# First weights in halves, later head tables, and a plan that knows where the rounded weights lie

## The chip, the cores and the metric

The kernel runs on one core of one Trainium2 chip. Its time is the device time of one execution in microseconds (us). The core has five engines that run their own instruction streams in order and wait for one another by semaphores: TensorE (PE in the profile; its weight loads are PEld), VectorE (DVE), ScalarE (ACT), GpSimd (POOL) and SyncE (SP), which issues DMAs.

## The reference, cut to what matters

Two layers of a streaming encoder run on 512 prompt rows and 64 sample rows of 1024 features with the same weights. The sample group has 1024 cached keys. In each layer:

```python
h = rms_norm(x, norm_g)
u_p, z_p, q, k, v, qi, ki, wi, z_a, g_p, g_a = split(h @ w_in)
br_pool = (pool_mix(u_p) * silu(z_p)) @ w_pool_out     # means over 2, 4, 8, 16 rows, mixed by groups
q, k, qi, ki = rope(q), rope(k), rope(qi), rope(ki)
score = sum_heads(wi * relu(qi . ki));  sel = top_k(score)      # 128 of the prompt's keys, 256 of the sample's
o = softmax(q . k[sel]) . v[sel]
br_attn = (o * silu(z_a)) @ w_attn_out
x = x + (sigmoid(g_p) * br_pool + sigmoid(g_a) * br_attn) @ w_o
```

After the second layer x is normed once more. The outputs are y, the new k, v and indexer keys, and the last rows of the pooling input.

## The kernel before

**Tiling.** Everything lies transposed: features on the 128 partitions, the 576 rows (T) along the free dimension, in two halves of 288. x is eight blocks of 128 x 576. A weight piece is a tile of 128 x 1024 (512 KB); a layer has 58 of them, and one piece makes one "block" of the product: eight steps k, each with three matmuls for each half of the rows. They make up an f32 product from rounded parts: high weights by high x, high weights by low x, low weights by high x (`step`). High parts are cast by ScalarE; the low part of x is a subtraction on VectorE. The low part of a weight piece is, from the third piece on, made by a DMA that GpSimd issues and that adds the raw tile to the negated high part (`split_to`). The first two pieces are rounded in halves: ScalarE casts 512 columns, then VectorE (first half) or GpSimd (second half) subtracts (`split_first`). Raw tiles (`raw`) and rounded tiles (`whl`) have three places each, so piece i + 2 is rounded into the place of piece i - 1.

**Order.** A Python planner writes the instruction streams out when the program is built. Main work is emitted in the order of `ORDER` (u, z, the gates gp with the pool output po, then k, q, v, then za, ga). Side work (pooling, scores, selection, attention, rounding of what comes next) is written as generators; after each step of a product `plan.pump()` looks which generators may go on. `need(engine, tiles)` says yes if by the plan's clocks the tiles are ready and, where a `room` is given, the engine's backlog is no more than that many microseconds. The plan's clocks are estimates of each engine's free time (`plan.free`), and `plan.wrote` and `plan.last` keep when a tile is written and last used. Tiles taken through `plan.slot` know when their place comes free; the `whl` tiles are not taken so. `plan.finish` pumps until given generators are done.

**Weights.** `weights()` hands out the next piece and loads three ahead. `block()` takes the piece, calls `split_to(i + 3)`, which puts the rounding of piece i + 2 into ScalarE's stream, and then emits the eight steps.

**The start of layer 0.** SP issues gains, the ki weights, x blocks 0 and 1, the whole first weight piece, x blocks 2 to 7. `arrive(k)` (line 1465) calls `first` (line 498): ScalarE scales block k into its high part, VectorE makes the low part; at k = 0 the ki weights are split (`ki_split`); at k = 1 the first weights are rounded; at k = 7 all eight blocks are squared on ScalarE and the squares summed by seven additions on VectorE. The loop of line 580 runs the ki product and the first product side by side; with `LAG` = (1, 2) the high-weight matmuls of step k - 1 and the low-weight matmuls of step k - 2 follow the ki matmuls of block k. Blocks 0 to 2 arrive ahead of the loop, and turn k brings block k + 2. At the end of turn 4 weight piece 1 is rounded (line 599), at the end of turn 6 piece 2. The second product (line 611 on) uses piece 1; after its third step come the norm's ten matmuls (`norm_a`), after its fifth the transposes that spread the result over Rt (`norm_b`). The rotary tables, and all that leaves a product, are multiplied by Rt.

**Head tables.** `head_tables` (line 968) loads the cosine and sine tables of the heads and multiplies them by Rt with two GpSimd instructions into Ct and St. It is started at the first gate block (gp 0, line 1324). k and q use the tables.

Nearly every instruction goes through the helper at line 262, so rows are told apart by tiles.

Of the kernel before, what the change touches and what calls it, by code (L numbers as in the profile page):

```python
# [10 lines left out]
F32 = mybir.dt.float32  # L11
F32R = mybir.dt.float32r
AF = mybir.ActivationFunctionType
OP = mybir.AluOpType

P = 128
# [30 lines left out]
UNITS = 3  # L47
FIRST_H = ()
LAG = (1, 2)
DMA_US = 3.0  # L50
WARM = 11
NORM_A = 0
# [215 lines left out]
def encoder_step(ctx: ExitStack, tc: tile.TileContext, a: dict):  # L268
# [60 lines left out]
    for l in range(DEPTH):  # L329
        pieces += [(l, j) for j in range(a["n_pieces"])]  # L330
    raw_of, split_of = {}, {}
    state = {"load": 0, "split": 0, "next": 0}

    def load_to(n):
        while state["load"] < min(n, len(pieces)):
# [3 lines left out]
            dma.dma_start(raw_of[i], a["w"][l, j])  # L339
            state["load"] += 1  # L340

    def split_to(n):
        while state["split"] < min(n, len(pieces)):
            i = state["split"]
            load_to(i + 1)
            x = raw_of.pop(i)
            w = rot.tile([P, 2, 1024], F32R, name="whl", tag="whl", bufs=3)
            act.copy(w[:, 0], x)

            act.activation(w[:, 1], x, AF.Copy, scale=-1.0)  # L350
            pool.dma_start(w[:, 1].bitcast(F32), x, accum_op=OP.add)
            plan.let(x)
            split_of[i] = w
            state["split"] += 1

    def split_first(i=0):

        load_to(i + 1)
        x = raw_of.pop(i)
        w = rot.tile([P, 2, 1024], F32R, name="whl", tag="whl", bufs=3)  # L360
        for c, eng in ((slice(0, 512), dve), (slice(512, 1024), pool)):
            act.copy(w[:, 0, c], x[:, c])
            eng.tensor_tensor(w[:, 1, c], x[:, c], w[:, 0, c].bitcast(F32), op=OP.subtract)
        plan.let(x)
        split_of[i] = w
        state["split"] = i + 1

    def weights():
        i = state["next"]
# [83 lines left out]
            if True in low:  # L453
                pe.matmul(o, lhsT=wl, rhs=h, start=False, stop=k == nk - 1)

    def product(ps, w, xh, xl, nk, off=0):
        for k in range(nk):
            step(ps, w, xh, xl, k, nk, off)
            plan.pump()

    def block(xh, xl, nk=8):
        w, i = weights()
        split_to(i + 3)
        ps = ps_mm()
        product(ps, w, xh, xl, nk)
        return ps

    class Entry:
# [29 lines left out]
        def first(self, k, x, ki_split):  # L498

            c = slice((k % 2) * T, (k % 2 + 1) * T)  # L500
            g = gains[:, self.l, k:k + 1]
            h = self.h[k // 2][:, c]
            if k in FIRST_H:
                dve.tensor_scalar(h, x, g, None, op0=OP.mult)
            else:
                act.activation(h, x, AF.Copy, scale=g)
            if k == 0:
                ki_split()
            dve.scalar_tensor_tensor(self.lo[k // 2][:, c], x, g, h.bitcast(F32), op0=OP.mult, op1=OP.subtract)
            self.rest.append(x)  # L510
            if k == 7:
                for i, x in enumerate(self.rest):
                    sq = tmp() if i else self.acc
                    act.activation(sq, x, AF.Square)
                    if i:
                        dve.tensor_tensor(self.acc, sq, self.acc, op=OP.add)
# [38 lines left out]
    def layer(l, x, arrive):  # L555
# [6 lines left out]


        if l == 0:
            for k in range(3):
                arrive(k)
        w, n = weights()
        if l:
# [11 lines left out]
        for k in range(8 + lag[1]):  # L580
            if k == 7:
                plan.finish(*x.coming)
            if 3 <= k + 2 < 8:
                arrive(k + 2)
            if k < 8:
                c = (k % 2) * T
                for s in range(2):
                    cols = slice(c + s * HT, c + (s + 1) * HT)
                    pe.matmul(ps_k[s][:, :HT], lhsT=kiw[:, k], rhs=xh[k // 2][:, cols], start=k == 0, stop=False)
                for s in range(2):  # L590
                    cols = slice(c + s * HT, c + (s + 1) * HT)
                    pe.matmul(ps_k[s][:, :HT], lhsT=kiw[:, k], rhs=xl[k // 2][:, cols], start=False, stop=k == 7)
            if lag[0] <= k < 8 + lag[0]:
                step(ps_q0, w, xh, xl, k - lag[0], 8, low=(False,))
            if k >= lag[1]:
                step(ps_q0, w, xh, xl, k - lag[1], 8, low=(True,))
                plan.pump()
            if l == 0 and k == 4:
                split_first(1)
            if l == 0 and k == 6:  # L600
                split_to(3)
# [718 lines left out]
        for name, i in ORDER:  # L1320
            if name == "k" and i == 0:
                att = start(attend(), 3)
            if name == "gp" and i == 0:
                start(head_tables(), 2)
            jobs[name](i)
        plan.finish(sel)
# [131 lines left out]
    for k in range(8):  # L1458
        if k % 2 == 0:
            xt.append(quart())  # L1460
        dma.dma_start(xt[-1][:, (k % 2) * T:(k % 2 + 1) * T], a["x"][k])
        if k == 1:
            load_to(1)

    def arrive(k):
        x.first(k, xt[k // 2][:, (k % 2) * T:(k % 2 + 1) * T], ki_split)
        if k == 7:
            plan.let(*xt)
        if k == 1:
            split_first()  # L1470

    x = layer(0, x, arrive)
    for l in range(1, DEPTH):
# [107 lines left out]
```

## Time and profile before

| what | us |
|---|---|
| median of 3 runs | 920.47 (920.26 to 920.74) |
| the profiled execution | 921.1 |
| its span, first to last instruction | 919.3 |
| TensorE busy | 894.8 |
| VectorE busy | 668.3 |
| ScalarE busy | 593.2 |
| GpSimd busy | 202.1 |

Engines work side by side, so busy times don't add up. A row of a timeline gives the start, how long the instruction (or the run of like instructions, x their number) took, the engine, the operation with what it writes and reads, and in brackets how long the engine had been idle before and what ended that. The granted clock of TensorE was 0.995 of full speed on average.

### The profile page before, as it was taken

Reading aid. Unit: us, or ns where it says so; the run is one execution under the profiler, and the core shown is the slowest. Engines: PE = TensorE matmul, PEld = TensorE weight load, DVE = VectorE, ACT = ScalarE, POOL = GpSimd, SP = SyncE. Lnnn points to the kernel's source line nnn. Section 1 sums busy time; section 2 is a strip of 40 time slices with the busy share of each in tenths; the row PEclk is TensorE's granted clock in tenths of the full one; section 3 lists DMA queues with packets and bytes.
Section 4 is the critical chain, followed back from the end, with each engine's and each line's share of the span. In section 5 each row is a group of like instructions: output and inputs, shape, how many; then the busy total and the mean of one; then the engine's idle time right before and its main releaser. Section 6 shows DMA issues by size and latency. Waiting matters only on the chain.

```text
span 919.3 us, 17403 instructions
## 1 busy us (share of the span) xinstructions
PE 894.8 (97%) x6613; PEld 881.4 (96%) x6613; DVE 668.3 (73%) x1554; ACT 593.2 (65%) x1056; POOL 202.1 (22%) x217
## 2 busy tenths in 40 slices
PE   8999999999999999999999999999999999999996
PEld 7999999999999999999999999999999999999995
DVE  6996899799896677362359779988989875755314
ACT  7556534588898975564537564446889988556642
POOL 3111211134432300112211121113443222011121
PEclk9999999999999999999999999999999999999998
DMA  7756587766555675779976667786655548648862
GB/s 266 187 140 164 134 214 189 173 161 160 125 145 147 179 199 150 186 202 240 263 191 175 154 151 163 191 203 180 165 139 133 157 124 221 189 135 222 236 146 104
DMA packets 54500, 160.97 MB, mean 175 GB/s; under 512 B 6736, under 2 KB 9040, under 8 KB 54416
## 3 DMA queue, kind: packets, MB, share of 16 engines
q0 software_dynamic: 16416, 59.78, 34.8%
q1 hardware_dynamic: 38000, 100.08, 32.2%
q8 instruction: 52, 0.85, 0.4%
q14 instruction: 32, 0.26, 0.1%
HBM read 85.37 MB, written 14.69 MB: 109 GB/s over the span
## 4 chain that ended last, share of the span: by engine, by line
PE 68%; DVE 14%; ACT 13%; issue 3%; DMA 1%; POOL 1%; SPq 0%; DVEq 0%; ACTq 0%; POOLq 0%
PE mm L262 57%; PE sm L262 11%; DVE tmp L262 6%; DVE quart L262 6%; ACT prob L262 4%; ACT whl L262 3%; ACT quart L262 2%; ACT qz L262 1%; ACT L262 1%; DVE big L262 1%; ACT tmp L262 1%; POOL tmp L262 1%; DMA raw<-in_w_dram 1%; DMA prob<-in_c_v_dram 1%; DVE prob L262 0%
## 5 line engine op out<-in xcount | busy, mean ns | idle before, releaser
L262 PE MATMUL mm<-quart,whl 128*128 128x288 f32 (+1 forms) x5568 | 780.4, 296 | 1.6 <-ACT quart L262 1.2
L262 PEld LDWEIGHTS mm<-quart,whl 128*128 128x128 f32 x5568 | 754.2, 188 | 4.3 <-ACT quart L262 2.0
L262 POOL DMA_DIRECT2D whl<-raw x114 | 99.3, 871 | 648.9 <-ACT whl L262 433.1
L262 ACT CAST whl<-raw 128x1024 fp32r<-128x1024 f32 (+1 forms) x118 | 121.8, 1034 | 133.2 <-PE mm L262 88.7
L262 ACT ACTIVATE whl<-raw 128x1024 fp32r<-128x1024 f32 x114 | 120.4, 1056 | 0.0
L262 ACT ACTIVATE prob<-prob,stat 128x128 f32<-128x128 f32 (+3 forms) x128 | 67.5, 554 | 6.8 <-DVE stat L262 6.4
L262 DVE SCALAR_TENSOR_TENSOR quart<-prob,wcol,quart 128x256 f32<-128x256 f32 (+4 forms) x60 | 42.1, 704 | 26.4 <-ACT prob L262 25.1
L262 ACT ACTIVATE prob<-sm 128x256 f32<-128x256 f32 (+4 forms) x72 | 33.5, 481 | 38.4 <-PE sm L262 38.4
L262 DVE MATCH_REPLACE8 quart<-stat,quart 128x256 f32<-128x256 f32 (+2 forms) x96 | 51.1, 539 | 0.0
L262 DVE MAX8 stat<-quart 128x8 f32<-128x256 f32 (+2 forms) x96 | 47.3, 541 | 0.0
L262 DVE MAX8 quart<-quart 128x8 f32<-128x544 f32 x64 | 46.3, 723 | 1.2
L262 DVE MATCH_REPLACE8 quart<-quart 128x544 f32<-128x544 f32 x64 | 45.4, 709 | 0.0
L262 DVE TENSOR_TENSOR tmp<-tmp 128x576 f32<-128x576 f32 (+7 forms) x62 | 44.3, 720 | 1.3
L262 DVE TENSOR_TENSOR quart<-quart 128x576 fp32r<-128x576 f32 (+6 forms) x30 | 26.4, 881 | 21.5 <-ACT quart L262 21.0
L262 DVE TENSOR_TENSOR big<-sm,big 128x512 fp32r<-128x512 f32 (+1 forms) x64 | 28.9, 483 | 16.3 <-ACT big L262 16.1
L262 ACT CAST quart<-tmp 64x512 fp32r<-64x512 f32 (+4 forms) x44 | 24.1, 566 | 22.0 <-POOL tmp L262 11.7
L262 ACT COPY prob<-sm 64x512 f32<-64x512 f32 (+1 forms) x24 | 12.3, 514 | 39.0 <-PE sm L262 38.6
L262 PE MATMUL sm<-quart,big 128*128 128x128 f32 (+3 forms) x176 | 32.2, 291 | 1.4 <-DVE tmp L262 1.4
L262 ACT CAST big<-sm 128x512 fp32r<-128x512 f32 (+2 forms) x72 | 28.0, 434 | 8.4 <-PE sm L262 8.0
L262 DVE SCALAR_TENSOR_TENSOR quart<-tmp,gains,quart 128x576 fp32r<-128x576 f32 x8 | 6.5, 818 | 31.6 <-ACT quart L262 31.6
L262 DVE CUSTOM_DVE_ANT_0 prob<-sm,quart 128x512 f32<-128x512 f32 (+2 forms) x48 | 25.8, 550 | 4.8 <-PE sm L262 4.8
L262 DVE TENSOR_TENSOR quart<-mm,tmp 128x576 f32<-128x576 f32 (+2 forms) x10 | 6.4, 638 | 29.3 <-PE mm L262 29.3
(157 smaller groups left out, 1025.5 us busy)
## 6 DMA issues: line engine op xcount, KB each, us to landing
raw<-in_w_dram SPq DMA_DIRECT2D x116, 512.0 KB, 4.9
whl<-raw POOLq DMA_DIRECT2D x114, 512.0 KB, 4.8
mp<-tmp SPq DMA_DIRECT2D x16, 288.0 KB, 3.3
tmp<-mp SPq DMA_DIRECT2D x16, 288.0 KB, 4.7
prob<-in_c_k_dram SPq DMA_DIRECT2D x16, 256.0 KB, 4.8
prob<-in_c_v_dram SPq DMA_DIRECT2D x16, 256.0 KB, 3.8
out_o_v_dram<-quart SPq DMA_DIRECT2D x8, 320.0 KB, 4.6
quart<-in_x_dram SPq DMA_DIRECT2D x8, 288.0 KB, 6.3
```

Source lines behind the costliest of these rows:

```text
L262: return f(*args, **kw)
```

## The change

It has four parts.

1. The first weight piece is fetched as two halves, one behind x block 1 and one behind x block 3, and each half is rounded when block 1 or block 3 has been scaled (`load_half`, `split_half`). Four blocks instead of three arrive ahead of the loop, and turn k brings block k + 3 instead of k + 2. The ki weights are split ahead of block 0's scaling.
2. The head tables are started at gate block `TABLES_AT` = 6 instead of 0.
3. `whls` makes the rounded tiles and tells the plan that a tile's place is free when the tile three before has been used for the last time.
4. In `block()`, the rounding of piece i + 2 is emitted after step `SPLIT_AT` = 0 and the pump behind it, instead of ahead of the eight steps.

```diff
 UNITS = 3
 FIRST_H = ()
 LAG = (1, 2)
+TABLES_AT = 6
+SPLIT_AT = 0
 DMA_US = 3.0
 WARM = 11
 NORM_A = 0
@@ -329,6 +331,7 @@
     for l in range(DEPTH):
         pieces += [(l, j) for j in range(a["n_pieces"])]
     raw_of, split_of = {}, {}
+    whl_names = []
     state = {"load": 0, "split": 0, "next": 0}
 
     def load_to(n):
@@ -339,12 +342,20 @@
             dma.dma_start(raw_of[i], a["w"][l, j])
             state["load"] += 1
 
+    def whls(i):
+
+        w = rot.tile([P, 2, 1024], F32R, name="whl", tag="whl", bufs=3)
+        whl_names.append(w.tensor.name)
+        if i > 2:
+            plan.wrote(w, plan.last[whl_names[i - 3]])
+        return w
+
     def split_to(n):
         while state["split"] < min(n, len(pieces)):
             i = state["split"]
             load_to(i + 1)
             x = raw_of.pop(i)
-            w = rot.tile([P, 2, 1024], F32R, name="whl", tag="whl", bufs=3)
+            w = whls(i)
             act.copy(w[:, 0], x)
 
             act.activation(w[:, 1], x, AF.Copy, scale=-1.0)
@@ -357,13 +368,33 @@
 
         load_to(i + 1)
         x = raw_of.pop(i)
-        w = rot.tile([P, 2, 1024], F32R, name="whl", tag="whl", bufs=3)
+        w = whls(i)
         for c, eng in ((slice(0, 512), dve), (slice(512, 1024), pool)):
             act.copy(w[:, 0, c], x[:, c])
             eng.tensor_tensor(w[:, 1, c], x[:, c], w[:, 0, c].bitcast(F32), op=OP.subtract)
         plan.let(x)
         split_of[i] = w
         state["split"] = i + 1
+
+    halves_of = (slice(0, 512), slice(512, 1024))
+
+    def load_half(c):
+
+        if c == 0:
+            raw_of[0] = raws()
+        dma.dma_start(raw_of[0][:, halves_of[c]], a["w"][0, 0, :, halves_of[c]])
+        state["load"] = 1
+
+    def split_half(c):
+        x, cols = raw_of[0], halves_of[c]
+        if c == 0:
+            split_of[0] = whls(0)
+        w, eng = split_of[0], (dve, pool)[c]
+        act.copy(w[:, 0, cols], x[:, cols])
+        eng.tensor_tensor(w[:, 1, cols], x[:, cols], w[:, 0, cols].bitcast(F32), op=OP.subtract)
+        state["split"] = 1
+        if c:
+            plan.let(raw_of.pop(0))
 
     def weights():
         i = state["next"]
@@ -453,16 +484,17 @@
             if True in low:
                 pe.matmul(o, lhsT=wl, rhs=h, start=False, stop=k == nk - 1)
 
-    def product(ps, w, xh, xl, nk, off=0):
+    def product(ps, w, xh, xl, nk, off=0, ahead=0):
         for k in range(nk):
             step(ps, w, xh, xl, k, nk, off)
             plan.pump()
+            if k == SPLIT_AT:
+                split_to(ahead)
 
     def block(xh, xl, nk=8):
         w, i = weights()
-        split_to(i + 3)
         ps = ps_mm()
-        product(ps, w, xh, xl, nk)
+        product(ps, w, xh, xl, nk, ahead=i + 3)
         return ps
 
     class Entry:
@@ -503,9 +535,9 @@
             if k in FIRST_H:
                 dve.tensor_scalar(h, x, g, None, op0=OP.mult)
             else:
+                if k == 0:
+                    ki_split()
                 act.activation(h, x, AF.Copy, scale=g)
-            if k == 0:
-                ki_split()
             dve.scalar_tensor_tensor(self.lo[k // 2][:, c], x, g, h.bitcast(F32), op0=OP.mult, op1=OP.subtract)
             self.rest.append(x)
             if k == 7:
@@ -562,7 +594,7 @@
 
 
         if l == 0:
-            for k in range(3):
+            for k in range(4):
                 arrive(k)
         w, n = weights()
         if l:
@@ -580,8 +612,8 @@
         for k in range(8 + lag[1]):
             if k == 7:
                 plan.finish(*x.coming)
-            if 3 <= k + 2 < 8:
-                arrive(k + 2)
+            if l == 0 and 4 <= k + 3 < 8:
+                arrive(k + 3)
             if k < 8:
                 c = (k % 2) * T
                 for s in range(2):
@@ -1320,7 +1352,7 @@
         for name, i in ORDER:
             if name == "k" and i == 0:
                 att = start(attend(), 3)
-            if name == "gp" and i == 0:
+            if name == "gp" and i == TABLES_AT:
                 start(head_tables(), 2)
             jobs[name](i)
         plan.finish(sel)
@@ -1459,15 +1491,15 @@
         if k % 2 == 0:
             xt.append(quart())
         dma.dma_start(xt[-1][:, (k % 2) * T:(k % 2 + 1) * T], a["x"][k])
-        if k == 1:
-            load_to(1)
+        if k in (1, 3):
+            load_half(k // 2)
 
     def arrive(k):
         x.first(k, xt[k // 2][:, (k % 2) * T:(k % 2 + 1) * T], ki_split)
         if k == 7:
             plan.let(*xt)
-        if k == 1:
-            split_first()
+        if k in (1, 3):
+            split_half(k // 2)
 
     x = layer(0, x, arrive)
     for l in range(1, DEPTH):
```

## Rows read from the trace of the kernel before

**Rows 1.** The page's busy times: engine, busy us, share of the span, instructions.
```profile
PE 894.8 (97%) x6613; PEld 881.4 (96%) x6613; DVE 668.3 (73%) x1554; ACT 593.2 (65%) x1056; POOL 202.1 (22%) x217
```

**Rows 2.** Busy time by stage: stretch, length, busy us of each engine, PEclk, DMA.
```profile
0.00:45.00 45.00, 40.35 (x268) 37.89 (x269) 35.31 (x73) 28.07 (x48) 11.82 (x24) 1.00 0.77 231
45.00:420.00 375.00, 370.07 (x2752) 365.59 (x2751) 292.10 (x691) 254.97 (x463) 82.35 (x84) 1.00 0.66 166
...
880.00:919.30 39.30, 30.14 (x227) 29.57 (x225) 13.65 (x30) 13.01 (x22) 7.46 (x5) 0.89 0.45 126
```

**Rows 3.** The chain of waits over the first 30 us: start, us, what.
```profile
2.60 5.59 DMA raw<-in_w_dram
...
10.07 1.34 DVE quart L262
...
11.97 0.79 PE mm L262 x6
...
23.03 1.28 PE sm L262 x10
```

**Rows 4.** Busy times from 8 to 13 us; the last column is GB/s by DMA.
```profile
8.00:13.00 5.00, 3.74 (x22) 2.87 (x22) 3.90 (x6) 4.52 (x7) 1.28 (x1) 1.00 1.04 401
```

**Rows 5.** Timeline of ScalarE at the start.
```profile
13.98 1.15 ACT L262 CAST whl<-raw 128x512 fp32r<-128x512 f32 x2 [1.25 <-DMA raw<-in_w_dram]
15.03 0.77 ACT L262 ACTIVATE quart<-quart,gains 128x576 fp32r<-128x576 f32 x1
...
16.29 4.12 ACT L262 ACTIVATE tmp<-quart 128x576 f32<-128x576 f32 x7
```

**Rows 6.** Timeline of VectorE at the start.
```profile
10.07 4.24 DVE L262 SCALAR_TENSOR_TENSOR quart<-quart,gains 128x576 fp32r<-128x576 f32 x5 [0.51 <-ACT quart L262]
14.64 0.69 DVE L262 TENSOR_TENSOR whl<-raw,whl 128x512 fp32r<-128x512 f32 x1 [0.33 <-ACT whl L262]
15.84 1.28 DVE L262 SCALAR_TENSOR_TENSOR quart<-quart,gains 128x576 fp32r<-128x576 f32 x1 [0.51 <-ACT quart L262]
17.05 5.93 DVE L262 TENSOR_TENSOR acc<-tmp,acc 128x576 f32<-128x576 f32 x7
```

**Rows 7.** Timeline of GpSimd at the start.
```profile
15.21 1.30 POOL L262 TENSOR_TENSOR whl<-raw,whl 128x512 fp32r<-128x512 f32 x1 [4.43 <-ACT whl L262]
```

**Rows 8.** Timelines of GpSimd, VectorE and TensorE from 93 to 100 us.
```profile
93.94 1.75 POOL L262 TENSOR_TENSOR Ct<-tmp,Rt 128x576 f32<-128x576 f32 x1
...
94.07 3.56 DVE L262 SCALAR_TENSOR_TENSOR quart<-prob,wcol,quart 128x512 f32<-128x512 f32 x1 [1.80 <-ACT prob L262]
...
99.26 0.74 DVE L262 SCALAR_TENSOR_TENSOR quart<-prob,wcol,quart 128x512 f32<-128x512 f32 x1
...
98.97 0.50 PE L262 MATMUL sm<-quart,big 128*128 128x512 f32 x1 [0.70 <-DVE tmp L262]
```

**Rows 9.** Timelines of VectorE and GpSimd from 203 to 220 us.
```profile
208.78 0.73 DVE L262 MAX8 quart<-quart 128x8 f32<-128x544 f32 x1
...
208.59 1.30 POOL L262 TENSOR_TENSOR quart<-quart 128x512 fp32r<-128x512 f32 x1
```

**Rows 10.** Timelines of ScalarE and TensorE around four stalls.
```profile
331.43 1.05 ACT L262 CAST whl<-raw 128x1024 fp32r<-128x1024 f32 x1 [3.12 <-PE mm L262]
...
335.78 0.63 PE L262 MATMUL sm<-ident,quart 128*128 128x128 f32 x4 [1.20 <-DVE quart L262]
...
784.12 0.63 PE L262 MATMUL sm<-ident,quart 128*128 128x128 f32 x4 [1.20 <-DVE quart L262]
...
321.09 0.33 PE L262 MATMUL sm<-ident,prob 128*128 128x128 f32 x1 [0.81 <-ACT prob L262]
...
219.50 0.77 PE L262 MATMUL sm<-ident,tmp 128*128 128x128 f32 x5 [0.91 <-ACT tmp L262]
```

**Rows 11.** Timelines of VectorE and ScalarE at the attention's end.
```profile
377.82 0.29 DVE L262 TENSOR_TENSOR quart<-prob,quart 128x128 fp32r<-128x128 f32 x1 [0.87 <-ACT quart L262]
...
381.76 1.05 ACT L262 CAST whl<-raw 128x1024 fp32r<-128x1024 f32 x1 [3.97 <-PE mm L262]
```

## The prediction

> **What bounds the kernel now.** Read first the busy times of the page: TensorE works for 894.8 of 919.3 us [rows 1], so every engine but TensorE counts only where TensorE stands still: 24.5 us. Next a table by stage: of that idle time 4.65 us lie before 45 us, 4.93 us between 45 and 420 us, and 9.16 us after 880 us [rows 2]; the second layer repeats the first's stalls, as its copy of one of them shows [rows 10]. The change touches neither the arithmetic of TensorE nor the stretch after 880 us, so at most the first kind (the start, once) and the second (twice) can move. Then, for the start, the chain of waits and the timelines of three engines [rows 3 to 7]; for the middle, the timeline around each stall [rows 8 to 11].
>
> **The start.** In the kernel before, the first weights land at 2.60 + 5.59 = 8.19 us, ScalarE rounds them ahead of x block 2, and VectorE's low part of block 2 ends at 10.07 + 1.34 = 11.41 us; from there on TensorE is hardly idle until the norm's matmuls at 23.03 us [rows 3]. Where x lands isn't recorded apart; I work it out. Weights 1 landed at 13.98 us, since ScalarE waited for them [rows 5], and the queue moves 401 GB/s [rows 4]: 512 KiB take 1.31 us, a block of x (288 KiB) 0.74 us, half a weight tile 0.65 us. So block 7 lands at 12.7, block 4 at 10.5, block 2 at 9.0 us. With the weights in halves, block 2 passes one half: 9.0 - 0.65 = 8.35 us; block 3 comes at 9.1, the second half at 9.75, and blocks 4 to 7 and weights 1 stay where they are.
>
> Gain: block 2 is scaled by 8.35 + 0.77 = 9.1 us (0.77 as for block 7 [rows 5]) and its low part takes at most 0.8 us (five low parts took 4.24 us, the first of them 1.34 [rows 3, 6]): 9.9 us instead of 11.4. TensorE then has the same 66 matmuls of the first product and the ki product ahead of it, 6 in 0.79 us or 0.132 each [rows 3], and ends them 1.5 us sooner, near 18.9 us.
>
> Loss: `arrive(7)` now comes at k = 4, one turn sooner, and so ahead of `split_first(1)`, which stays at the end of turn 4. Block 7 brings along all eight squares (ScalarE) and seven sums (VectorE). Before, weights 1 were rounded at 13.98 us and the squares followed; now they queue behind both. ScalarE: block 7 until 12.7 + 0.77 = 13.4, eight squares of 0.59 (seven took 4.12 us [rows 5]) until 18.1, the two casts until 19.25. VectorE: low part of block 7 until about 14.6 (14.3 without, 14.95 with an earlier block by GpSimd, below), seven sums of 5.93 us together [rows 6] until 20.5, and only then the low half of weights 1, 0.69 us. GpSimd's half, 1.30 us [rows 7], starts at 19.25, in the middle of the sums, and it stops VectorE when that reads two operands from SBUF: the low part that took 1.28 us stood beside such an instruction [rows 6, 7], and an instruction that takes 0.74 us took 3.56 while GpSimd ran two of 1.75 us [rows 8]. So 1.3 us more: the low half of weights 1 is ready at 20.5 + 1.3 + 0.69 = 22.5 us (20.95 without the stop, 22.9 with all of it). The third matmul of the second product needs it: TensorE stands from 19.2 to 22.5 us, what it won is gone, and more. After that come 16 matmuls (2.1 us) and the norm's ten (1.28 us): 25.9 us, where before it was 23.03 + 1.28 = 24.31 [rows 3]. Everything behind hangs on that norm, with the same instructions in the same order. Cost of the start: +1.6, between 0.0 and +2.0; I take **+1.5 us**.
>
> Other queues of the start: SP's third weight load waits for tile 0, which GpSimd frees some 1 us later, and the tables behind it come as much later; they are used after the norm, over 8 us on. The fourth load waits for tile 1, freed at 20.6 us instead of 16.5; its rounding comes near 29 us. Both are covered. Rounding ki ahead of block 0 costs ScalarE 0.4 us while it waits for x anyway.
>
> A rule weighed: the Trainium skill, "DMA: Bandwidth & Descriptors", section "Measured (HBM→SBUF, 128 partitions, SWDGE, issued from GpSimd)", asks for transfers of 1 MiB or more and gives 138 GB/s for 64 KB and 341 GB/s for 1 MB. By it (an estimate at 240 GB/s) each half would take 1.1 us instead of 0.65, blocks 4 to 7 would land 0.9 us late, and the start would cost +2.4 us. The trace does not bear it out for transfers queued one behind another: blocks of 288 KiB flowed at 401 GB/s [rows 4].
>
> **The head tables.** They are made at the seventh gate block instead of the first, so their two GpSimd instructions (the one shown, the other right behind it), their two loads and their issues move by eight or nine blocks. Today they lie on VectorE's sums of the scores: 3.56 us where 0.74 is the price, and TensorE waits 0.70 us for VectorE right after [rows 8], likewise in layer 1. At the new place VectorE runs the search for the largest (MAX8, MATCH_REPLACE), which is not stopped: a MAX8 beside GpSimd took 0.73 us [rows 9], and products that read PSUM. TensorE has no stall there to make longer. The users come three blocks later, over 15 us for a load of 5 us and two instructions of 1.75. Idle time of 0.70 is read between the modelled ends of matmuls, which overlap a little; I take 0.8 a layer: **-1.6 us** (0 to -2).
>
> **The planner.** Two edits act together on the order of everything between 45 and 880 us. The plan now knows that a weight tile's place is free only when TensorE has done with the tile three before; and the rounding is put into ScalarE's queue after the first step of a block and what that step released. Where it matters can be seen: at 331.43 us ScalarE's rounding waits 3.12 us for TensorE, the exponential of the sample's logits goes behind it, and TensorE stands 1.20 us for its transposes, in both layers [rows 10]. The plan took ScalarE for free up to 3 us sooner than it was; with the wait known, either the exponential goes first or the transposes are put later. Saving 0 to -2.4; I take -2.0. At 321.09 us TensorE stands 0.81 us for a probability row that ScalarE had behind a rounding [rows 10]; there the rounding had not waited for TensorE, so only its later place helps: half of 2 x 0.81, -0.8. The 0.91 us for the transposes of v [rows 10] come from a ScalarE that was busy throughout; 0. Rounding starts one step later, 6 matmuls or 0.8 us; a tile is used two blocks on, over 12 us, against 2.1 us of rounding and 5 of GpSimd's transfer: covered. But a new order can also make new stalls; the trace can't show them, so I bound what the planner does by losing and by winning 3 us beside what I take. Planner: **-2.8 us**, from 0 to -6, with new stalls +3.
>
> **Sum.** The profiled execution took 921.1 us; +1.5 - 1.6 - 2.8 = -2.9 gives 918.2. The median of the runs is 0.6 below the profiled one: **917.5 us**, faster by 3.0.
>
> **Rivals.**
> A, the forecast, chance 0.42.
> B, the planner's order is only another order: stalls go and come. +1.5 - 1.6 = -0.1: 920.4 us. For it: most stalls of the middle stand where ScalarE was busy anyway. Chance 0.27.
> C, all three stalls of [rows 10] go in both layers: 2 x (1.20 + 0.81 + 0.91) = 5.8 in place of 2.8: 914.5 us. Against it: the third doesn't hang on the rounding. Chance 0.13.
> D, the start wins: if the squares don't hold up weights 1, TensorE keeps its 1.5 us: -1.5 - 1.6 - 2.8: 914.5 us. Against it: the program order. Chance 0.08.
> E, slower: ScalarE, now known to be busy, is offered less work, so the attention ends later. Today its last piece is ready at 377.82 + 0.29 = 378.1 us, and the product that needs it starts at about 381.7 [rows 11]: 3.6 us in hand per layer. From there on each microsecond counts twice. If it ends 6 us later: 2 x 2.4 + 1.5 - 1.6 = +4.7: 925 us. For it: the plan's rule that refuses work while ScalarE's backlog is over 1 us now applies after every rounding. Against it: VectorE has 2.8 us more for the search. Chance 0.10.
>
> **Numbers.** About 0.2% (1.8 us) is what a measurement tells from no change: below 918.6 is faster, above 922.3 slower. Faster: A 0.36, C and D 0.21, B 0.05: 0.62. Same: A 0.06, B 0.19, E 0.02: 0.27. Slower: B 0.03, E 0.08: 0.11. The range runs from 913.6 (C and D with a little more) to 921.8 (B with the start's full cost); A alone lies in 915.5 to 919.5.
>
> **What would show it.** Start right: TensorE stands about 3 us near 20 us, waiting for VectorE's low half of weights 1, after eight squares on ScalarE; wrong: the second product runs through, and the norm's matmuls come before 23 us. Tables right: no stall near 99 and 547 us. Planner right: idle time between 45 and 420 us, without the tables' share, falls from 4.2 to some 3 us. The forecast fails if a stall of several microseconds appears at the attention's end.

## The result, and the profile after

The changed kernel took 910.79 us (median of 4 runs, 908.78 to 912.5) against 920.61 us for the kernel before beside it (920.26 to 921.6): a ratio of 0.9891, 95% interval 0.9869 to 0.9913. That is 9.8 us less by the medians, where 3.0 were forecast; the range ended at 913.6. The profiled execution took 911.28 us, with a span of 909.5. One run of e11_best below took 3162.86 us and one of the kernel before 1631.54, and the ratios leave both out.

The page's busy times of the kernel after, beside [rows 1]:

```profile
PE 892.2 (98%) x6613; PEld 882.1 (97%) x6613; DVE 663.2 (73%) x1554; ACT 594.4 (65%) x1056; POOL 200.3 (22%) x217
```

The number of instructions is the same on each of these engines; TensorE's idle time fell from 24.5 to 17.3 us. The table by stage of the kernel after (columns as in [rows 2]) shows where:

```profile
0.00:45.00 45.00, 38.08 (x250) 36.37 (x251) 33.01 (x67) 27.55 (x43) 12.19 (x24) 0.96 0.72 221
45.00:420.00 375.00, 374.86 (x2795) 371.51 (x2794) 294.20 (x701) 257.51 (x471) 81.37 (x85) 1.00 0.67 170
...
500.00:880.00 380.00, 379.84 (x2836) 376.56 (x2835) 283.56 (x675) 258.81 (x459) 84.43 (x86) 1.00 0.69 176
```

From 45 to 420 us TensorE stands 0.14 us, where it stood 4.93 [rows 2]; from 500 to 880 us 0.16, where the same view of before gives 4.96. The start got worse: 6.92 us idle instead of 4.65, at a mean clock of 0.96. So the middle gave more than was ever put on it, and the start took part of that back. Three fixed points of the program, the last of them its end, price both: the 24-matmul product of the start began at 37.27 us and now begins at 40.03 (+2.8); layer 1's entry came at 484.82 and comes at 481.49 us; so layer 0 after the start gained 2.8 + 3.3 = 6.1 us, and the rest of the program 9.8 - 3.3 = 6.5.

The middle before, as TensorE's list of waits from 150 to 420 us (what waited, for whom: us in total, times, longest), a view not shown ahead of the prediction:

```profile
PE sm L262 <- DVE quart L262: 1.4, 2, 1.2
PE sm L262 <- ACT tmp L262: 0.9, 1, 0.9
PE sm L262 <- ACT prob L262: 0.8, 1, 0.8
PE sm L262 <- ACT quart L262: 0.8, 2, 0.5
PE sm L262 <- DVE big L262: 0.2, 1, 0.2
```

The same list of the kernel after is empty. ScalarE at the place of the first stall of [rows 10] in the kernel after:

```profile
322.94 1.21 ACT L264 ACTIVATE quart<-quart,stat 128x1088 f32<-128x1088 f32 x1
...
325.38 1.05 ACT L264 CAST whl<-raw 128x1024 fp32r<-128x1024 f32 x1
```

The exponential (322.94) now goes ahead of the rounding (325.38), and the rounding that waited 3.12 us for TensorE [rows 10] waits for nothing. TensorE runs through:

```profile
320.20 6.55 PE L264 MATMUL mm<-quart,whl 128*128 128x288 f32 x48
326.58 0.60 PE L264 MATMUL sm<-ident,quart 128*128 128x128 f32 x4
```

The start after: TensorE, then ScalarE, VectorE and GpSimd (they answer to [rows 3, 5 to 7]).

```profile
22.30 3.92 PE L264 MATMUL mm<-quart,whl 128*128 128x288 f32 x16 [2.97 <-DVE whl L264]
26.05 1.18 PE L264 MATMUL sm<-ones,acc 128*128 128x1 f32 x10
...
10.60 3.04 ACT L264 ACTIVATE quart<-quart,gains 128x576 fp32r<-128x576 f32 x4
...
14.11 4.12 ACT L264 ACTIVATE tmp<-quart 128x576 f32<-128x576 f32 x7
18.14 2.07 ACT L264 CAST whl<-raw 128x512 fp32r<-128x512 f32 x3
...
14.82 6.82 DVE L264 TENSOR_TENSOR acc<-tmp,acc 128x576 f32<-128x576 f32 x7
21.56 0.68 DVE L264 TENSOR_TENSOR whl<-raw,whl 128x512 fp32r<-128x512 f32 x1
...
19.34 1.69 POOL L264 TENSOR_TENSOR whl<-raw,whl 128x512 fp32r<-128x512 f32 x1 [7.38 <-ACT whl L264]
```

The squares go ahead of the casts of weights 1, and the sums ahead of their low half, which ends at 22.24 us; TensorE waits for it. That is the stall foretold for 19.2 to 22.5 us. What follows it is slower than foretold: 16 matmuls in 3.92 us instead of 2.1. The clock in the table by stage of that stretch:

```profile
22.30:24.00 1.70, 1.70 (x8) 1.70 (x9) 1.40 (x4) 1.49 (x2) 0.20 (x1) 0.57 0.58 77
24.00:26.00 2.00, 2.00 (x10) 2.00 (x10) 0.00 (x0) 0.00 (x0) 1.43 (x2) 0.52 1.11 260
26.00:28.00 2.00, 2.00 (x19) 2.00 (x18) 0.57 (x4) 0.21 (x1) 0.00 (x0) 1.00 1.01 264
```

PEclk is the third column from the end: after 3 us without a matmul the clock is granted at about half (1.2 of 2.4 GHz) from 22.3 to 26 us, then whole again.

### The profile page after: what moved, and what is told of

It is laid out like the page before. It is cut to its first block, busy times and chain, and to the rows that moved or that the text cites. A ratio compares the mean times of both kernels' runs of the same rounds, so it can differ in the third digit from the quotient of the medians.

```text
span 909.5 us, 17417 instructions
## 1 busy us (share of the span) xinstructions
PE 892.2 (98%) x6613; PEld 882.1 (97%) x6613; DVE 663.2 (73%) x1554; ACT 594.4 (65%) x1056; POOL 200.3 (22%) x217
## 4 chain that ended last, share of the span: by engine, by line
PE 86%; DVE 6%; ACT 4%; DMA 2%; issue 1%; POOL 1%; SPq 0%; DVEq 0%; POOLq 0%; ACTq 0%
PE mm L264 72%; PE sm L264 14%; DVE tmp L264 3%; DVE quart L264 2%; DMA whl<-raw 1%; ACT prob L264 1%; ACT quart L264 1%; ACT whl L264 1%; POOL tmp L264 1%; DMA quart<-in_x_dram 1%; ACT qz L264 0%; ACT L264 0%; ACT tmp L264 0%; SPq L264 0%; DVE rcol L264 0%
## 5 line engine op out<-in xcount | busy, mean ns | idle before, releaser
L264 ACT ACTIVATE prob<-prob,stat 128x256 f32<-128x256 f32 (+3 forms) x128 | 67.7, 555 | 4.7 <-DVE stat L264 4.2
L264 DVE SCALAR_TENSOR_TENSOR quart<-prob,wcol,quart 128x256 f32<-128x256 f32 (+4 forms) x60 | 36.4, 609 | 28.6 <-ACT prob L264 27.5
L264 DVE TENSOR_TENSOR tmp<-tmp 128x576 f32<-128x576 f32 (+7 forms) x62 | 42.4, 688 | 1.3
L264 DVE TENSOR_TENSOR tmp<-mm,tmp 128x576 f32<-128x576 f32 x28 | 21.0, 750 | 29.8 <-PE mm L264 29.5
L264 ACT ACTIVATE tmp<-quart 128x576 f32<-128x576 f32 (+2 forms) x24 | 14.4, 639 | 22.4 <-DVE quart L264 22.4
```

Source lines behind the costliest of these rows:

```text
L264: return f(*args, **kw)
```

## The experiments

All times are medians, each beside runs of the kernel before on the same chip; "idle" is TensorE's between 45 and 420 us (4.93 in the kernel before). For the middle five theories were tried: (1) the plan's knowledge of the tile's place frees it; (2) the rounding's new place does; and of what the place does, (3) it lets what the first step released into ScalarE's queue ahead of 2 us of rounding, (4) it is simply later, or (5) it works as more margin in the plan would. For the start: the order ahead of weights 1, and the clock after the wait.

**The four parts alone**, each put into the kernel before.

e1_plan, the plan's knowledge (part 3):

```
-            w = rot.tile([P, 2, 1024], F32R, name="whl", tag="whl", bufs=3)
+            w = whls(i)        # the new tile, with plan.wrote(w, plan.last[whl_names[i - 3]])
...
```

> The kernel before, and only the plan's knowledge of the three places (part 3). Theory 1, that this knowledge is what empties the middle of stalls: TensorE's idle time between 45 and 420 us falls from 4.93 to under 1.5 us and the time by 6 us or more (ratio below 0.994). Theory 2, that the later place of the rounding does it (part 4): within 2 us of before. A gain between the two, some 3 us, says that both are needed.

920.72 us, ratio 0.9993 (0.9981 to 1.0004); idle 4.14 us. No gain that can be told from none. TensorE's stalls of over half a microsecond between 150 and 420 us:

```profile
197.37 0.38 PE L262 MATMUL sm<-quart,qz 128*128 128x256 f32 x1 [0.86 <-DVE stat L262]
...
321.75 0.33 PE L262 MATMUL sm<-ident,prob 128*128 128x128 f32 x1 [0.80 <-ACT prob L262]
...
353.57 1.10 PE L262 MATMUL sm<-big,qzs 128*128 128x364 f32 x5 [0.64 <-DVE big L262]
```

The 1.20 us at 335.78 [rows 10], which the prediction put on the unknown place, are gone, and so are the 0.91 at 219.50; but 0.86 and 0.64 us have come elsewhere, and the stall at 321 us stays. (Of the 4.14 us, 0.70 are the head tables' stall, which this kernel keeps.)

e2_step, the rounding's place (part 4):

```
-    def product(ps, w, xh, xl, nk, off=0):
+    def product(ps, w, xh, xl, nk, off=0, ahead=0):
...
             step(ps, w, xh, xl, k, nk, off)
             plan.pump()
+            if k == 0:
+                split_to(ahead)
...
-        split_to(i + 3)
...
-        product(ps, w, xh, xl, nk)
+        product(ps, w, xh, xl, nk, ahead=i + 3)
```

> The kernel before, and only the rounding put behind a block's first step (part 4), the plan still ignorant of the places. Theory 2: 6 us or more faster, idle time of TensorE from 45 to 420 us under 1.5 us. Theory 1: within 2 us of before, since the plan still takes ScalarE for free while it waits for a place.

911.54 us, 0.9888 (0.9873 to 0.9903); its table by stage:

```profile
45.00:420.00 375.00, 374.27 (x2789) 370.66 (x2789) 294.96 (x695) 257.54 (x468) 81.11 (x84) 1.00 0.66 170
...
500.00:880.00 380.00, 379.07 (x2826) 375.34 (x2826) 284.86 (x671) 257.20 (x458) 84.26 (x86) 1.00 0.68 175
```

Idle falls to 0.73 and 0.93 us, nearly all of it the head tables' stall, which this kernel keeps. This one edit, without the plan's knowledge, is the whole gain: theory 1 falls, theory 2 stands.

e3_tables (part 2), the head tables at the seventh gate block:

```
-            if name == "gp" and i == 0:
+            if name == "gp" and i == 6:
```

> The kernel before, and only the head tables started at gate block 6 (part 2). As priced in the prediction: 1.6 us faster (0 to 2), the stalls near 99 and 547 us gone and the others in their places. Rival, that the plan's order around them changes as well: the other stalls move, and the time by more than 2 us either way.

918.95 us, 0.998 (0.997 to 0.999), idle 4.20: the stalls near 99 and 547 us are gone, the others stand.

e4_start, part 1 alone (the kernel after with parts 2 to 4 undone):

> The kernel before, and only the start (part 1: halves, four blocks ahead, ki first). Theory that the start is a loss: the norm's matmuls end 2.9 us later than before, as in the changed kernel, with a stall near 20 us and the clock at half behind it, and the time is 2.5 to 3.2 us longer (ratio about 1.003). Rival, that the start's loss is won back where TensorE waits for other engines later: less than 1 us longer.

924.42 us, 1.0037 (1.0024 to 1.0049). TensorE stands before the second product as in the kernel after:

```profile
22.00 2.39 PE L264 MATMUL mm<-quart,whl 128*128 128x288 f32 x16 [2.93 <-DVE whl L264]
```

In this execution the clock stayed whole (16 matmuls in 2.39 us; the norm's end at 25.40 us), and it was the fastest of ten, 922.32, which is 1.5 over the median of the kernel before; the slowest took 926.62. Not all of that is the start: one stall of the second layer, 0.81 us in the kernel before (769.43 us), is 1.77 here. By the ratios the four parts give -0.6, -10.3, -1.8 and +3.4 us, together -9.3; the kernel after has 0.0109 of 921, -10.0. They add up within the intervals.

**Where the rounding stands.** e5, e6 and e15 change the kernel after, e16 and e10 the kernel before.

e5_before_pump: still after the first step, but ahead of what that step releases.

```
             step(ps, w, xh, xl, k, nk, off)
-            plan.pump()
             if k == SPLIT_AT:
                 split_to(ahead)
+            plan.pump()
```

> The changed kernel, with the rounding after the first step as there, but ahead of that step's pump instead of behind it. Theory 3, that what counts is that work released at a block's border goes into ScalarE's stream ahead of 1.9 us of rounding: most of part 4's gain is lost, TensorE's stalls of 0.5 to 1.2 us between 200 and 420 us are back, and the time is 5 us or more over the changed kernel's 910.8 (ratio to before above 0.995). Theory 4, that what counts is the 0.8 us by which the rounding comes later, so that ScalarE no longer stands before a place that TensorE still holds: within 2 us of the changed kernel.

920.42 us, 1.0002 (0.9986 to 1.0018); idle 3.39. TensorE's list of waits from 150 to 420 us:

```profile
PE sm L264 <- DVE stat L264: 0.8, 1, 0.8
PE sm L264 <- DVE big L264: 0.8, 2, 0.6
PE sm L264 <- ACT prob L264: 0.8, 1, 0.8
PE sm L264 <- ACT quart L264: 0.8, 2, 0.5
```

These are e1's stalls: the same list of e1 has the same six waits, each within 0.02 us and about 1 us earlier. So the step's delay by itself gives nothing that can be seen; that e5 stands less than the 4.20 us of e3 comes from the plan's knowledge, which it shares with e1. The swap of these two lines gives the other 3.25 us (3.39 to 0.14), and about 10 us of the run (ratio 1.0002 against 0.9891). Theory 4 falls, theory 3 is borne out for this order. One of its stalls, ScalarE first, then TensorE:

```profile
320.38 1.03 ACT L264 CAST whl<-raw 128x1024 fp32r<-128x1024 f32 x1
321.31 1.05 ACT L264 ACTIVATE whl<-raw 128x1024 fp32r<-128x1024 f32 x1
322.27 0.39 ACT L264 ACTIVATE prob<-prob,stat 128x128 f32<-128x128 f32 x1
...
322.71 0.33 PE L264 MATMUL sm<-ident,prob 128*128 128x128 f32 x1 [0.80 <-ACT prob L264]
```

The 0.39 us that TensorE waits for stand behind 2 us of rounding that nobody needs for two blocks. The kernel before has the same picture at 318.75 us, ahead of its stall at 321.09 [rows 10], and again at 331.43, where the exponential stands behind the pair (ScalarE):

```profile
318.75 1.03 ACT L262 CAST whl<-raw 128x1024 fp32r<-128x1024 f32 x1
...
320.65 0.39 ACT L262 ACTIVATE prob<-prob,stat 128x128 f32<-128x128 f32 x1
...
333.34 1.19 ACT L262 ACTIVATE quart<-quart,stat 128x1088 f32<-128x1088 f32 x1
```

Of its stalls of 0.15 us and more between 150 and 420 us, 3.0 of 4.0 us wait for something close behind such a pair: the two of 0.81 and 1.20 us, and three of 0.19, 0.30 and 0.48. The kernel after has no such stall.

e16_pump, the kernel before with what is already released let in ahead of the rounding, at the block's border:

```
+        plan.pump()
         split_to(i + 3)
```

> The kernel before, with one pump put ahead of the rounding at a block's border, and nothing else. Theory 3, that the order at the border is what counts: part of the gain, 2 to 6 us, since some of the border's work is not yet ready there and is let in only by the first step's pump. If it is the place behind the first step as such: within 2 us of before.

921.86 us, 1.0008 (0.9998 to 1.0018); idle 4.94. To let in what is ready at the border isn't enough; 2 to 6 us were expected by theory 3.

e6_step3, the rounding after the fourth step (`SPLIT_AT = 3`):

> The changed kernel with SPLIT_AT = 3: the rounding behind the fourth step of a block. Theory 3: the border's work still goes first, so the gain stays within 2 us; what could be lost is a weight tile that is rounded too late (it has more than 12 us, minus 2.4). Theory 4: likewise within 2 us. Rival to both, that the first step's position was a lucky order and any other order brings stalls back: 4 us or more over the changed kernel.

924.11 us, 1.0025 (1.0008 to 1.0042); idle 3.56 (in the fastest of ten executions, 919.98 us, the one profiled). Its longest stall, ScalarE and TensorE:

```profile
268.27 1.05 ACT L264 CAST whl<-raw 128x1024 fp32r<-128x1024 f32 x1
...
270.19 0.49 ACT L264 ACTIVATE prob<-prob,stat 128x256 f32<-128x256 f32 x1
...
271.61 0.44 PE L264 MATMUL sm<-ident,prob 128*128 128x128 f32 x2 [1.85 <-ACT prob L264]
```

Later isn't better: at this stall the rounding falls in front of the next pieces. Theory 3 was expected to keep the gain here within 2 us, and it didn't.

e15_step1, after the second step (`SPLIT_AT = 1`):

> The changed kernel with SPLIT_AT = 1: the rounding behind the second step. Theory 3, with its refinement that the rounding must not stand in front of work in flight within the block: between the first step's 910.8 and the fourth's 924.1, nearer to the first, 911 to 916. By luck: no order in the three places; 917 or more is as likely as not.

919.52 us, 0.9976 (0.996 to 0.9992); idle 2.77 (in the slowest of ten executions, 922.71 us). By theory 3, 911 to 916 were expected.

e10_cut, the kernel before with the rounding in two: the cast at the border, the negated copy and its transfer after the fourth step:

```
-        split_to(i + 3)
+        split_a(i + 3)       # load, act.copy(w[:, 0], x)
...
+            if k == 3:
+                split_b()    # negated copy, accumulating transfer
```

> The kernel before, with the rounding cut in two: the cast ahead of a block's first step as before, the negated copy and GpSimd's transfer behind the fourth step. Theory 3, that the waits are 1.9 us of rounding in front of what TensorE waits for: no piece stands in front for more than 0.95 us, so the stalls behind it (0.81 and 1.20 us near 321 and 336 us, 0.48 near 250 us) shrink by half or go, and the time falls by 3 to 6 us. Rival, that each new position of ScalarE's work brings its own stalls, as with the rounding behind the fourth step: within 2 us of before or slower.

918.21 us, 0.996 (0.9945 to 0.9975). The stalls near 321 and 336 us go, one of 1.25 us comes at 249.4 for another ScalarE piece. With half of the pair moved behind released work, about a third of the gain is there.

**The plan's margin.** `MARGIN` (0.4 us) is how long before the plan's present the inputs of a TensorE piece must be there. e9_margin: the kernel before with 1.6.

> The kernel before, with MARGIN = 1.6 instead of 0.4: the plan gives TensorE a matmul on side work only when its operands have been ready for 1.6 us by the plan's clocks. Theory 5, that the stalls of the middle come from a plan that takes ScalarE for 1 to 2 us ahead of what it is, so that TensorE is sent too early to whatever stands behind a rounding: its idle time from 45 to 420 us falls below 2 us and the time by 5 us or more (ratio below 0.9945), with the rounding at its old place. Theory 3, that the rounding ahead of the border's work makes that work late, whatever TensorE does meanwhile: within 3 us of before.

937.93 us, 1.0173 (1.0146 to 1.02): the attention comes late, with one wait of 4.3 us in its course in the first layer, and idle 7.90. Theory 5 falls for this margin; no run tried a smaller step of it in the kernel before. e12_step3_margin, the kernel after with `SPLIT_AT = 3` and margin 1.6:

> The changed kernel with the rounding behind the fourth step (which lost the gain: 924.1) and MARGIN = 1.6. Theory 5: the margin heals this position too, TensorE's idle time from 45 to 420 us falls from 3.56 to under 1.5 us, and the time comes within 3 us of the changed kernel's 910.8. Theory 3: stays above 917.

959.01 us, 1.0405 (1.0385 to 1.0425), idle 15.1: worse than either edit alone.

e13_margin5 and e14_margin3, the kernel after with margins of 0.5 and 0.3, ask how far the stall-free middle hangs on one order:

> The changed kernel with MARGIN = 0.5 instead of 0.4, which redraws the order of the side work a little. If the place behind the first pump is good by its mechanism, TensorE's idle time from 45 to 420 us stays under 1.5 us and the time within 3 us of the changed kernel's 910.8. If it was a lucky order, stalls come back: 3 us of idle time or more in the stretch, and 916 us or more.

> The changed kernel with MARGIN = 0.3. By the mechanism: within 3 us of the changed kernel's 910.8, idle time under 1.5 us from 45 to 420 us (some more may come from the smaller margin itself). By luck: 916 us or more.

0.3: 917.32 us, 0.995 (0.9931 to 0.9969), idle 0.28; the middle is nearly whole. Its last matmuls come 6.4 us later than in the kernel after (909.24 for 902.80): 2.6 us of that are lost at the start (below), and 2.9 at the end, from the last norm's first matmuls on (896.82 for 893.28), where TensorE waits 2.53 us for ScalarE and the clock is at half. 0.5: 922.62 us, 1.0016 (1.0002 to 1.0029), idle 3.51, with two stalls of more than 1 us (ScalarE's row first, then TensorE's):

```profile
286.79 0.40 ACT L264 ACTIVATE prob<-prob,stat 128x128 f32<-128x128 f32 x1 [2.50 <-DVE stat L264]
...
288.56 0.33 PE L264 MATMUL sm<-ident,prob 128*128 128x128 f32 x1 [1.30 <-ACT prob L264]
...
306.80 1.25 PE L264 MATMUL sm<-big,quart 128*128 128x512 f32 x7 [1.55 <-DVE big L264]
```

Neither stands behind a rounding: before the first, ScalarE itself waited 2.50 us for VectorE. So the place takes away the stalls behind roundings, but how much of the 10 us stays hangs on the order that the plan happens to make: 0.1 us in its margin takes it all back, as a lucky order was expected to do. On the other side, six of the seven kernels with the rounding right behind the first step's pump and a margin of 0.5 or less (the one after, e2, e7, e8, e11 and e14; not e13) stand 0.13 to 0.73 us in the stretch, and each of the others 2.77 or more. That isn't six independent orders, since e7, e8 and e11 change only the start.

**The start.** e7_squares: the kernel after, squares and sums moved behind `split_first(1)`:

```
                 split_first(1)
+                arrive(8)     # the squares and sums, no longer in arrive(7)
...
```

> The changed kernel, with the eight squares and seven sums put behind the rounding of weight piece 1 (block 7 is still scaled in turn 4). Theory that the start's loss is this order alone: no stall of 3 us before the second product, the norm's matmuls end near 22.9 to 23.5 us (before 24.3, changed 27.2), and the time is 3.7 to 4.5 us below the changed kernel: ratio to before 0.984 to 0.986. Rival, that the wait passes to the sums, which then end as late as now did the low half: less than 2 us below.

908.11 us, 0.9862 (0.9847 to 0.9877). The second product follows at once, and TensorE waits for the sums instead:

```profile
17.28 4.40 PE L264 MATMUL mm<-quart,whl 128*128 128x288 f32 x32
22.74 1.28 PE L264 MATMUL sm<-ones,acc 128*128 128x1 f32 x10 [1.06 <-DVE acc L264]
```

The norm's matmuls end at 24.0 us, not 27.2.

e8_warm: the kernel after with matmuls added into a PSUM tile that nothing reads, in the wait:

```
+        if l == 0:
+            ps = ps_s()
+            for _ in range(7):
+                nc.tensor.matmul(ps[:, :P], lhsT=mask0, rhs=mask0, start=True, stop=True)
```

> The changed kernel, with seven matmuls on a constant tile (3.0 us) put into TensorE's stream where it waits for the low half of weights 1; nothing reads their result. Theory that 1.8 us of the start's loss come from TensorE's clock, which stood at half after 3.2 us without work: the 16 matmuls after the wait take 2.1 us instead of 3.9, PEclk stays 1.00, and the time falls by 1.5 to 2 us against the changed kernel. Rival, that the clock falls for another reason, or that the extra matmuls push the product back: within 0.7 us of it.

909.66 us, 0.988 (0.9866 to 0.9895):

```profile
17.87 1.72 PE L649 MATMUL sm<-mask 128*128 128x128 f32 x14
...
21.49 2.38 PE L264 MATMUL mm<-quart,whl 128*128 128x288 f32 x16 [1.64 <-DVE whl L264]
```

The same wait for the same weights, but the 16 matmuls behind it take 2.38 us, not 3.92, at a granted clock of 1.00. So 1.5 us of the start's cost in the profile after are the clock's. That the added matmuls kept it whole isn't shown: it stayed whole in e4 and e6 without them, and by their times e8 and the kernel after can't be told apart (0.988 and 0.9891, with intervals that overlap). (In this execution the sums began 0.8 us sooner than in the profile after; that part is no gain of the edit.)

e11_best: e7 with the squares of blocks 0 and 1 in ScalarE's waits for x:

```
+        if k == 1:
+            x.squares(0, 1)
...
+            x.squares(1, 2)
```

> The kernel with the squares behind the rounding of weights 1, and further the squares of x blocks 0 and 1 in the two stretches in which ScalarE waited for DMA (6.2 to 6.9 and 7.5 to 8.4 us). Two squares and one sum less on the way to the norm: its matmuls start 0.8 to 1.1 us sooner, the stall of 1.06 us ahead of them goes, and the time is 0.7 to 1.1 us below that kernel's 908.1: ratio to before 0.984 to 0.986. Rival, that the squares push block 2's scaling back by as much: no change.

907.05 us (three runs), 0.9842 (0.9821 to 0.9862); the best version here. The wait before the norm is gone too:

```profile
21.67 1.28 PE L264 MATMUL sm<-ones,acc 128*128 128x1 f32 x10
```

The halves of the first weights do give 1.4 us, once nothing stands ahead of weights 1: the norm ends at 22.95 us, and before at 24.31 [rows 3].

## Why the prediction was wrong

**The step that failed** is the planner's term, "-2.8 us, from 0 to -6", in both its size and its cause. The prediction put -2.0 of it on the plan knowing that the place wasn't free ("with the wait known, either the exponential goes first or the transposes are put later") and -0.8 on the rounding's later place. The runs turn that round: the knowledge alone gives -0.6 (interval -1.7 to +0.4), the place alone -10.3 (-8.9 to -11.7). What was said of the knowledge came true as far as it went (e1 has no stall at 336 us), but the stalls that a new order makes, which the prediction had bounded and not counted, ate it. What it gave as its sign, idle time from 4.2 to some 3 us, came out as 0.14. The rows were read rightly one by one: at 331.43 us the exponential did stand behind the rounding, and with the wait known that stall went. The error was to stop at the 3.12 us wait ahead of the rounding [rows 10]: the pair's own 2 us hold up the queue also where it hasn't waited, as at 318.75 us. Seen so, [rows 10] have one cause in two of their three stalls, and the same cause stands at three smaller ones that the prediction left out.

**Its bound was too narrow too.** The largest saving counted was rival C's: three stalls, 2.92 us a layer. The list of waits above has 4.1 us, and the whole went. And a microsecond of idle time was priced at a little over one: e3 took 0.73 us a layer out of the idle time and 1.8 us out of the run, e2 8.2 us (both layers) and 10.3. By these medians idle time read between modelled ends is some 1.25 times as dear (1.1 to 1.4 by e2's interval; e3's, 0.6 to 1.9, says little), and in the profile after layer 0 gained 6.1 us for 4.8 of idle time. By that, 2 x 4.1 x 1.25 = 10.3 us was there to be saved. C (914.5, chance 0.13) was the nearest, right that all stalls go and wrong in its price.

**The start** was right in mechanism and nearly in place: the stall (19.2 to 22.5 us foretold, ended at 22.3), its cause, and GpSimd stopping VectorE's sums (6.82 us where [rows 6] have 5.93: 0.9, for 1.3 foretold). The size was off: +1.5 forecast, norm's end 25.9; it came at 26.05 + 1.18 = 27.23, +2.9 (e4: +3.4, 2.2 to 4.5). The term left out is the clock after the stall: with a whole clock the same matmuls took 1.5 us less (e8), and the norm ended at 25.40 us (e4), near the forecast. Block 7 of x was scaled by 10.60 + 3.04 = 13.64 us, 13.4 foretold, so the halves didn't hold x up. By the rule of the Trainium skill that was weighed ("DMA: Bandwidth & Descriptors", section "Measured (HBM→SBUF, 128 partitions, SWDGE, issued from GpSimd)") it would have been an estimated 0.9 us later; this trace doesn't agree with it for halves queued among other transfers. Rival D (the order doesn't matter) was wrong in the kernel after; with the order mended it is nearly right: the norm ends 0.3 us sooner than before in e7 and 1.4 in e11.

**The head tables**: -1.6 forecast, -1.8 measured (-0.9 to -2.8). VectorE's sum of the scores that took 3.56 us [rows 8] takes 0.75 in the kernel after:

```profile
97.91 0.75 DVE L264 SCALAR_TENSOR_TENSOR quart<-prob,wcol,quart 128x512 f32<-128x512 f32 x1 [2.20 <-ACT prob L264]
```

**Rival B** (only another order) fell for the change, but holds for most of its neighbours: e5, e6, e13, e15 and e16 are 0.998 to 1.003. **Rival E** (attention late) fell: no wait at the attention's end. e9 shows it come true, +16 us, when the plan is really made to hold work back.

**What stays open.** Why the stalls that don't stand behind a rounding went as well (the 0.91 us at 219.50 [rows 10]), why e13 has new ones and e1 and e5 share theirs, and why the release at the border (e16) brings nothing by itself. Theory 3 also missed what it foretold for e6, e15 and e16. The order is made anew by each edit, and no run changed one piece of it and left the rest; so that the place of the rounding is the cause is shown for this plan's order (e2, e5), and that the queue behind the rounding is the whole reason is argued from the rows.

## What to carry to other kernels

In a kernel that one engine bounds, look at what stands in a helper's queue right ahead of each piece that the bound engine waits for: long work with slack (here 2 us of rounding, due two blocks later) belongs behind what the last step released, and the swap of two lines was worth some 10 of 920 us in this kernel (e5). But with a slightly larger margin in the plan the same place brought nothing (e13). Sum all the stalls of the stretch, not the three longest, when you bound what a new order can save. A greedy plan's order jumps: try its neighbours (the margin, the step) before you call a gain the edit's own.

## What the runs showed of the chip

- TensorE's granted clock at the start is not the same from profile to profile. Behind the same wait of 2.88 to 2.97 us in dense work, it is at about half for some 4 us in three profiles (after, e5, e13), for some 9 us in two (e14, e15), and it stays whole in three (e4, e6, e12). TensorE's rows with a margin of 0.3 (e14) are:

```profile
22.13 4.21 PE L264 MATMUL mm<-quart,whl 128*128 128x288 f32 x16 [2.97 <-DVE whl L264]
...
28.13 3.23 PE L264 MATMUL mm<-quart,whl 128*128 128x288 f32 x12
...
42.65 1.56 PE L264 MATMUL mm<-quart,whl 128*128 128x288 f32 x10 [1.35 <-DVE tmp L264]
```

The mean clock up to 45 us is 0.89 there, and the next product comes at 42.65 us, not 40.03. The clock also fell where no such wait stands: in e1, whose start is the one before, it is 0.67 from 24 to 29 us, behind a wait of 0.62 us, and 12 matmuls take 3.11 us where they take 1.84 in the kernel before:

```profile
23.75 3.11 PE L262 MATMUL mm<-quart,whl 128*128 128x288 f32 x12
```

Which it will be, no run here foretells. The spread between runs doesn't tell it either: 908.78 to 912.5 us after and 922.32 to 926.62 in e4, with the wait; 906.95 to 907.61 in e11, but 919.89 to 923.82 in 25 runs of the kernel before beside e1 to e4, without it.
- GpSimd and VectorE: two GpSimd products of some 1.75 us lay on a VectorE sum that took 3.56 us where 0.74 is usual [rows 8]; seven sums beside one GpSimd subtraction of 1.69 us took 0.9 us more than without. MAX8, with one input, wasn't stretched beside GpSimd [rows 9]. The Trainium skill, "SBUF — State Buffer", section "SBUF: two separate sides", says that the two share a port pair, held as a whole by a GpSimd operation or by a VectorE operation with two SBUF inputs; these rows agree.
